# A ring of eight weight places instead of five, a stream of modulation weights loaded two ahead, and its dot products kept in program order up to the scan

## The chip, the cores and the metric

The kernel runs on one core of a Trainium2 chip. The core has a matrix engine (PE, TensorE), a vector engine (DVE), a scalar engine (ACT), GpSimd (POOL), and SyncE (SP), which in this kernel issues most DMA transfers. Each engine takes its instructions in the order of its own queue and waits on semaphores for the others. On-chip memory is SBUF, 128 partitions; matmul results go to PSUM.

The metric is the device time in microseconds of one execution; the median of several runs counts.

## The reference, cut to what matters

One layer on 256 latent tokens with 256 context tokens ahead of them, model width 2048: a modulated RMS norm, one wide projection that feeds latent attention (MLA, 8 heads) and a bidirectional gated DeltaNet (8 heads, chunks of 64), gates, an output projection, and then a gated convolution MLP (FFN).

```python
sh1, sc1, g1, sh2, sc2, g2 = jnp.split(jax.nn.silu(c) @ w_ada[l] + b_ada[l], 6, axis=-1)
...
(lq_a, lkv_a, lk_r, ldq, ldk, ldv, ldz, lda, ldb, lga, lgb) = split_columns(
    modulate(rmsnorm(x, norm_mix[l]), sh1, sc1) @ w_in[l])
...
y_mla_l = attend_latent(q_l, k_l, v_l, k_c, v_c)
...
o_dn_l, _ = dn_bidirectional(lq, lk, lv, lgd, lbeta, s_ctx, True)
y_l = merge_branches(y_mla_l, dn_output(o_dn_l, ldz, dn_o_norm[l], x.dtype), lga, lgb,
                     w_o_mla[l], w_o_dn[l], w_out[l])
x = x + jnp.expand_dims(g1, -2) * y_l
x = x + jnp.expand_dims(g2, -2) * conv_glu(
    modulate(rmsnorm(x, norm_ffn[l]), sh2, sc2), w_ffn_up[l], ffn_conv[l], w_ffn_down[l])
```

Of the six modulation vectors the first two are needed at once. The other four (g1, sh2, sc2, g2) are first needed behind the output projection. The change touches how these four are computed: 4 x 2048 dot products over 2048 inputs, 64 MB of weights.

## The kernel before

**Weights.** All weights come from HBM as float32 tiles of 128 x 1024 (512 KB) and are split in two parts for the matmul. `raw_w` (L125) takes a place of the ring "raw" (NR = 5 places of 4 KB per partition) and issues the load on SP. For each half of 512 columns `split` (L119) then makes `whi` by a cast on ACT (L121) and `wlo = raw - whi` on DVE (L122); both come from rings of NH = 6. PE multiplies with `whi` and `wlo` (all matmuls have the line of the wrapper, L68). A place of "raw" comes free when the last `wlo` of its tile is done; SP then issues the next load that has been waiting for a place.

**The late modulation.** `ada_rest` (L254) is a generator with 128 steps. Step i takes one tile `rawa` of in_wada from the same ring "raw", and one DVE instruction (L279) multiplies it by the activated conditioning vector `sch` and sums along the row into a column of `parts`. In the trace this instruction shows as CUSTOM_DVE_ANT_0, followed by a short read of the accumulator. The load of step i + 1 is issued ahead of the dot product of step i (`ahead = load(0)`, then `ahead = load(i + 1)`), so at most one load is ahead of the dot product in the traced program. Every 32 steps one of the four vectors is finished (`ada.done`).

The generator is wrapped in a `Side`, which is advanced by a budget in nanoseconds: each step costs 1300. The head phase calls `ada(c * ADB / 22600)` (L804), the attention `ada(AD * c)` (L1166, AD = 0.55), the scan `ada(ADS * c)` (L1375, ADS = 0.3), and the output projection and the FFN call it with further budgets.

**Phases by the trace.** Projections and the DeltaNet's heads with their short convolutions and triangular systems run until about 440 us, then the attention (four pairs of heads, `mla_project` and `mla_attend`) until about 720, the scan of the DeltaNet (eight steps) until about 930, the output of both branches with their gates and the output projection until about 1063, a short norm, and the FFN to the end. While one of these runs, PE's queue is filled with projection matmuls of other parts (gates, in_wgm and in_wgd, product `gtp`).

**What sets the order.** The program is traced in Python. `pe`, `oact`, `odve` and `osync` are wrappers (class `Ordered`, L58ff): an instruction issued through one of them while it is `pinned` keeps its place behind the instruction of that engine that was traced ahead of it. Instructions issued through the plain `act`, `dve`, `sync` can be placed elsewhere on their engine by a scheduler that works with its own estimates. L279 is issued through `dve`, so its place is the scheduler's choice.

**Names that the text uses.** In a head's normalisation `row_diag` (L175): `l2m` (norms, then a power on POOL, L173), `rb_h` and `rb_l` (high and low part, L179 and L180), `rb_d` (diagonal, L185), which the matmul `bp` needs. In the attention: `ks` (column sums of squares on PE), `km` (L1022, DVE), the softmax row maximum `s_`/`mns` (L1118 to L1122), `PT` (the transposed weights, split) and `yps` (values). `zx` are gate rows. In the scan: `S` (state; scaled on ACT at L1311, copied at L1322), `jit`, `tt`, `yraw` and `gt` (the scan's own loads).

Of the kernel before, what the change touches and what calls it, by code (L numbers as in the profile page):

```python
# [11 lines left out]
ALU = mybir.AluOpType  # L12
# [14 lines left out]
G3 = 96 + 256 * N1  # L27
GR = 1024
GH = 512
NR = 5  # L30
NH = 6
AD = 0.55
GD0 = 2
# [20 lines left out]
def hybrid_block(ctx: ExitStack, tc: tile.TileContext, io, dbg=None):  # L54
    nc = tc.nc
    act, dve, pool, sync = nc.scalar, nc.vector, nc.gpsimd, nc.sync
# [18 lines left out]
    pe, oact, odve = (Ordered(e) for e in (nc.tensor, nc.scalar, nc.vector))  # L75
# [27 lines left out]
    half = const.tile([P, 1], F32, name="half")  # L103
# [20 lines left out]
    def raw_w(src):  # L124
        n = src.shape[1]  # L125
        raw = wr.tile([P, GR], F32, tag="raw", name="raw", bufs=NR)[:, :n]
        sync.dma_start(raw, src)
# [126 lines left out]
    def ada_rest():  # L254


        def load(i):
            w = wr.tile([P, GR], F32, tag="raw", name="rawa", bufs=NR)
            c, n = divmod(i, 32)
            sync.dma_start(w, io["wada2"][c, (n // 16 + c) % 2, n % 16])  # L260
            return w

        parts = ad.tile([P, 2, 16], F32, name="parts")
        half, ahead = None, load(0)
        for i in range(128):
            c, n = divmod(i, 32)
            h, j = (n // 16 + c) % 2, n % 16
            if h != half:

                for _ in range(1 if i else 0):  # L270
                    yield 1300
                half, sch = h, ad.tile([P, GR], F32, tag="sch", name="sch")
                sync.dma_start(sch, Sc[h])
                for _ in range(3):
                    yield 1300
            w = ahead
            if i < 127:
                ahead = load(i + 1)
            dve.tensor_tensor_reduce(out=w, in0=w, in1=sch, scale=1.0, scalar=0.0, op0=ALU.mult, op1=ALU.add, accum_out=parts[:, h, j : j + 1])  # L279
            if n == 31:  # L280
                cs = slice(16 * c, 16 * c + 16)
                dve.tensor_tensor(out=adaT[:, cs], in0=parts[:, 0], in1=parts[:, 1], op=ALU.add)
                dve.tensor_tensor(out=adaT[:, cs], in0=adaT[:, cs], in1=bada[:, 32 + 16 * c : 48 + 16 * c], op=ALU.add)
                ada.done = c + 1
            yield 1300
# [43 lines left out]
    def load_shift(p):  # L329
        raws = []  # L330
        for m in range(4):
            raws.append(wr.tile([P, GR], F32, tag="raw", name="raw", bufs=NR))
            osync.dma_start(raws[m], io["wadab"][p, m])
# [76 lines left out]
    def load(*what):  # L410
        for kind, n in what:
            d, f = {"w": (wts, load_scale), "s": (shifts, load_shift), "g": (grs, load_first)}[kind]
            d[n] = f(n)
# [204 lines left out]
    for st in range(8):  # L618
        B = [pg2.tile([P, 8, 64], F32R, tag=f"B{n}", name="B") for n in range(2)]
        for n in range(2):  # L620
            dve.tensor_tensor(out=B[n], in0=mle64.unsqueeze(1).broadcast_to([P, 8, 64]),
                              in1=ghl[:, n, st].unsqueeze(2).broadcast_to([P, 8, 64]), op=ALU.mult)
# [147 lines left out]
    def head_inputs(h, side=lambda c: None):  # L770
        if h < N1:
            xs = [dkx[:, 2 * h], dkx[:, 2 * h + 1]]
        else:
            xs = []
            for w in ("wdk", "wdv"):
                pss = proj(io[w][h], (0, 1), side)
                x = pb2.tile([P, 2, T], F32, tag="cx", name="cx")
                for s in range(2):
                    gather(pss[s], P, x[:, s])
                xs.append(x)  # L780
        ps = proj(io["wdq"][h], (0,), side)[0]
        xq = pb2.tile([P, 1, T], F32, tag="cq", name="cq")
        gather(ps, P, xq[:, 0])
        return xs[0], xs[1], xq

    ada = Side(ada_rest())
    ada.done = 0
    ins = {h: head_inputs(h) for h in (3, 0)}

    def chains(*hs):  # L790
# [412 lines left out]
    def branch(w, wh, f, ymat, out):  # L1203

        if f % 4 == 0:
            gt = pd2.tile([P, 4, T], F32, tag="gt", name="gt")
            sync.dma_start(gt, Gs[wh, :, f : f + 4])
            gts[wh] = gt
        W = load_w(io[w][f])
        ps = psm.tile([P, 512], F32, tag="mm", name="brp")  # L1210
        for k in range(HEADS):
            mm_hl(ps, P, W(k * P), ymat[:, k], k == 0, k == HEADS - 1)
            if k == 3:
                yield 1300
        ox = pd2.tile([P, T], F32, tag="ox", name="ox")
        act.activation(ox, ps[:, T:], AF.Copy, scale=0.5)
        dve.scalar_tensor_tensor(out=ox, in0=ps[:, :T], scalar=0.5, in1=ox, op0=ALU.mult, op1=ALU.add)
        dve.scalar_tensor_tensor(out=out, in0=gts[wh][:, f % 4], scalar=1.0, in1=ox, op0=ALU.add, op1=ALU.mult)
        yield 1300
# [143 lines left out]
    def e_fill():  # L1363
        for f in range(KD):
            for n in range(4):
                c = next(gates, None)
                if c is not None:
                    yield c
            yield from branch("womla", 0, f, YM, t1[:, f])

    fill = Side(e_fill())
    pe.pinned = True
    for c in scan():
        fill(RE * c)
# [234 lines left out]
```

## Time and profile before

| what | value |
|---|---|
| median of 3 runs | 1796.3 us (1796.25 to 1796.43) |
| the profiled execution | 1796.66 us |
| its span | 1794.8 us |
| granted TensorE clock, mean | 0.988 |
| ACT's casts to whi (L121) | 940, 574.3 us |
| DVE's wlo (L122) | 940, 632.6 us |
| L279, dot products | 128, 155.8 us |
| HBM read and written | 388.57 MB and 28.84 MB |

The span runs from the first to the last instruction in the trace. The engines work side by side, so their busy times don't add up to it. A group of instructions in the profile is named by line, engine and operation, with output and inputs by the program's names; the number behind the bar is its busy time, the next the mean duration in ns, and behind the second bar stands the time for which the engine stood idle just before them and who ended that.

### The profile page before, as it was taken

To read this page: it belongs to the slowest core of one execution; us is meant where nothing else is said; L and a number is where in the kernel's file an instruction comes from. 1 tells how busy PE (TensorE), PEld (TensorE's weight loads), DVE (VectorE), ACT (ScalarE), POOL (GpSimd) and SP (SyncE) were. 2 spreads that over 40 slices of the span, in tenths; PEclk is the share of its full clock that TensorE was granted. 3 is DMA by queue.
4 is the path that set the end of the run, shared out by engine and by line. 5 is a ranking of instruction groups with operands and counts; after the bars stand their busy time and mean duration, and the time that the engine had idled before them with its cause. 6 is when DMAs were issued, how large, how long until landed. Compare 5 with 4: busy or idle time off the path is not lost.

```text
span 1794.8 us, 34114 instructions
## 1 busy us (share of the span) xinstructions
PE 1740.9 (97%) x12957; PEld 1504.6 (84%) x12957; DVE 1353.9 (75%) x2692; ACT 944.5 (53%) x1962; POOL 42.1 (2%) x49
## 2 busy tenths in 40 slices
PE   7999999999999999899999989999999999999999
PEld 6787888887888888687878878888888888888888
DVE  4687899879677777576789889887788888755554
ACT  3334544444567666564655546555555555544443
POOL 0000010000000000000010000000000000000000
PEclk9999999999899999999999989999999999999999
DMA  9982788773778767888957966777677777666663
GB/s 383 399 319 89 207 241 241 228 213 104 220 241 260 229 213 249 279 308 309 317 166 240 327 234 224 244 229 229 190 224 226 225 225 225 184 199 199 198 199 122
DMA packets 191493, 419.79 MB, mean 234 GB/s; under 512 B 57248, under 2 KB 97312, under 8 KB 188896
## 3 DMA queue, kind: packets, MB, share of 16 engines
q1 hardware_dynamic: 164144, 402.38, 69.0%
q10 hardware_dynamic: 27184, 15.23, 2.8%
q8 instruction: 102, 1.67, 0.4%
q14 instruction: 63, 0.52, 0.1%
HBM read 388.57 MB, written 28.84 MB: 233 GB/s over the span
## 4 chain that ended last, share of the span: by engine, by line
PE 70%; issue 10%; DMA 9%; DVE 6%; ACT 3%; POOL 1%; SPq 0%; POOLq 0%; DVEq 0%; ACTq 0%
PE fps L68 25%; PE dps L68 13%; PE mmp L68 9%; PE gtp L68 7%; PE fp L68 4%; DMA rawa<-in_wada 4%; DVE wlo L122 2%; PE brp L68 2%; DMA raw<-in_wadab 1%; PE amp L68 1%; DVE rawa L279 1%; DMA raw<-in_wgd 1%; ACT whi L121 1%; PE op L68 1%; DMA raw<-in_wz 1%
## 5 line engine op out<-in xcount | busy, mean ns | idle before, releaser
L122 DVE TENSOR_TENSOR wlo<-raw,whi 128x512 fp32r<-128x512 f32 (+1 forms) x940 | 632.6, 685 | 220.4 <-ACT whi L121 212.1
L121 ACT CAST whi<-raw 128x512 fp32r<-128x512 f32 (+1 forms) x940 | 574.3, 619 | 425.2 <-PE dps L68 113.7
L68 PE MATMUL fps<-H,whi 128*128 128x512 f32 x1376 | 475.1, 394 | 1.7 <-DVE H L1446 1.7
L68 PE MATMUL fps<-H,wlo 128*128 128x256 f32 x1376 | 372.3, 281 | 0.3 <-DVE wlo L122 0.3
L68 PEld LDWEIGHTS fps<-H,whi 128*128 128x128 f32 x1376 | 253.7, 189 | 53.3 <-issue 2.0
L68 PEld LDWEIGHTS fps<-H,wlo 128*128 128x128 f32 x1376 | 259.8, 189 | 7.8 <-DVE wlo L122 0.7
L68 PE MATMUL gtp<-h,whi 128*128 128x512 f32 x640 | 235.1, 404 | 7.4 <-ACT whi L121 7.1
L68 PE MATMUL mmp<-h,whi 128*128 128x512 f32 x640 | 227.1, 397 | 0.0
L68 PE MATMUL dps<-GB,whi 128*128 128x512 f32 (+1 forms) x595 | 195.7, 378 | 0.0
L279 DVE CUSTOM_DVE_ANT_0 rawa<-rawa,sch 128x1024 f32<-128x1024 f32 x128 | 155.8, 1220 | 45.5 <-DMA rawa<-in_wada 41.9
L68 PE MATMUL gtp<-h,wlo 128*128 128x256 f32 x640 | 176.0, 285 | 4.4 <-DVE wlo L122 4.2
L68 PE MATMUL mmp<-h,wlo 128*128 128x256 f32 x640 | 176.0, 281 | 0.6 <-DVE wlo L122 0.6
L68 PE MATMUL dps<-GB,wlo 128*128 128x256 f32 x560 | 154.1, 280 | 0.0
L68 PEld LDWEIGHTS gtp<-h,whi 128*128 128x128 f32 x640 | 121.8, 192 | 34.1 <-ACT whi L121 9.5
L68 PEld LDWEIGHTS mmp<-h,whi 128*128 128x128 f32 x640 | 119.0, 188 | 24.7 <-issue 0.4
L68 PEld LDWEIGHTS gtp<-h,wlo 128*128 128x128 f32 x640 | 122.9, 192 | 11.9 <-DVE wlo L122 7.5
L68 PEld LDWEIGHTS dps<-GB,whi 128*128 128x128 f32 x595 | 109.2, 188 | 21.1
L68 PEld LDWEIGHTS mmp<-h,wlo 128*128 128x128 f32 x640 | 120.3, 188 | 3.9 <-DVE wlo L122 1.3
L68 PEld LDWEIGHTS dps<-GB,wlo 128*128 128x128 f32 x560 | 105.1, 188 | 0.6
L68 PE MATMUL fp<-h,gh 128*128 128x256 f32 (+1 forms) x448 | 85.1, 290 | 2.5 <-ACT h L68 1.7
L68 PEld LDWEIGHTS fp<-h,gh 128*128 128x128 f32 (+1 forms) x448 | 69.4, 189 | 7.6 <-issue 4.1
L517 ACT COPY fx<-fps 128x256 f32<-128x256 f32 x86 | 31.8, 372 | 65.4 <-PE fps L68 65.3
(566 smaller groups left out, 2525.4 us busy)
## 6 DMA issues: line engine op xcount, KB each, us to landing
rawa<-in_wada SPq DMA_DIRECT2D x128, 512.0 KB, 4.7
raw<-in_wgate SPq DMA_DIRECT2D x82, 512.0 KB, 4.3
raw<-in_wval SPq DMA_DIRECT2D x82, 512.0 KB, 4.6
raw<-in_wdown SPq DMA_DIRECT2D x80, 512.0 KB, 4.3
wt<-in_wadas SPq DMA_DIRECT2D x16, 1024.0 KB, 10.8
raw<-in_wadab SPq DMA_DIRECT2D x32, 512.0 KB, 9.2
raw<-in_wgm SPq DMA_DIRECT2D x32, 512.0 KB, 4.7
raw<-in_wgd SPq DMA_DIRECT2D x32, 512.0 KB, 6.1
```

The costliest lines, as they stand in the source:

```text
L68: i = f(*a, **k)
L121: act.copy(hi, raw)
L122: dve.tensor_tensor(out=lo, in0=raw, in1=hi, op=ALU.subtract)
L279: dve.tensor_tensor_reduce(out=w, in0=w, in1=sch, scale=1.0, scalar=0.0, op0=ALU.mult, op1=ALU.add, accum_out=parts[:, h, j : j + 1])
L517: act.copy(out, ps[:M, T:])
```

## The change

The ring "raw" gets eight places (NR = 8). Room for them, 12 KB more per partition, comes from a scratch area that is cut to 1024 (`dynamic_dma_scratch_size`). `ada_rest` starts with two loads and keeps two ahead of the dot product. The dot product goes through `odve` while `ada.bound` is true, that is until the line just ahead of the scan's loop, and through `dve` from there on. The line numbers behind the last edits move by one.

```diff
-NR = 5
+NR = 8
...
-        half, ahead = None, load(0)
+        half, ahead = None, [load(0), load(1)]
...
-            w = ahead
-            if i < 127:
-                ahead = load(i + 1)
-            dve.tensor_tensor_reduce(out=w, in0=w, in1=sch, ...)
+            w = ahead.pop(0)
+            if i < 126:
+                ahead.append(load(i + 2))
+            (odve if ada.bound else dve).tensor_tensor_reduce(out=w, in0=w, in1=sch, ...)
...
-    ada.done = 0
+    ada.done, ada.bound = 0, True
...
     fill = Side(e_fill())
+    ada.bound = False
     pe.pinned = True
     for c in scan():
...
-    nc = bacc.Bacc("TRN2", target_bir_lowering=False, num_devices=1)
+    nc = bacc.Bacc("TRN2", target_bir_lowering=False, num_devices=1, dynamic_dma_scratch_size=1024)
```

The change moves instructions on DVE, ACT and SP; every engine has the same instructions as before, and PE's order is the same but for seven small places. Three places follow, each with the rows of before first.

**DVE in the attention, second pair of heads, ahead of the first km.** Each row is a line, an operation, output and inputs, and the shape; a dot product is the row ISA rawa,parts (L279 before, L68 where it goes through the wrapper), with its short second part behind it.

```order
L518 TENSOR_TENSOR zx<-gtp,zx 128x256
L279 ISA rawa,parts<-rawa,sch 128x1024
L279 ISA parts 128x1
L917 SCALAR_TENSOR_TENSOR zx<-zt,zx 128x256
L122 TENSOR_TENSOR wlo<-raw,whi 128x512
L1118 ISA s__6299,mns<-kbc,sps 128x512
L1118 ISA mns 128x1
L122 TENSOR_TENSOR wlo<-raw,whi 128x512
L1120 TENSOR_SCALAR mns<-mns,qm 128x1
L279 ISA rawa,parts<-rawa,sch 128x1024
L279 ISA parts 128x1
L1022 SCALAR_TENSOR_TENSOR km<-ks,krm 128x4
```

```order
L518 TENSOR_TENSOR zx<-gtp,zx 128x256
L122 TENSOR_TENSOR wlo<-raw,whi 128x512
L917 SCALAR_TENSOR_TENSOR zx<-zt,zx 128x256
L122 TENSOR_TENSOR wlo<-raw,whi 128x512
L1118 ISA s__6301,mns<-kbc,sps 128x512
L1118 ISA mns 128x1
L1120 TENSOR_SCALAR mns<-mns,qm 128x1
L1022 SCALAR_TENSOR_TENSOR km<-ks,krm 128x4
L990 CAST rb_h<-km 128x4
L1122 RECIPROCAL mns<-mns 128x1
```

Before, one dot product stands behind the first zx and one directly ahead of km. Now none stands in this stretch, and the next one follows behind the reciprocal and km. Just ahead of the stretch there were three dot products between the first wlo and the reciprocal, two of them next to each other, and there are two now.

**SP and ACT at the entry to the scan.** SP's loads of in_wgd (gate weights), in_womla and in_wada, the stores Ys of the attention and the first of the scan's own loads (jit):

```order
L127 DMA raw<-in_wgd 128x1024 x6
L127 DMA raw<-in_womla 128x1024
L1140 DMA Ys<-ryx 128x256
L260 DMA rawa<-in_wada 128x1024
L1238 DMA jit<-KTs 128x1024
L1140 DMA Ys<-ryx 128x256
L1239 DMA jit<-Vs 128x1024
```

```order
L127 DMA raw<-in_wgd 128x1024 x6
L127 DMA raw<-in_womla 128x1024
L1140 DMA Ys<-ryx 128x256
L260 DMA rawa<-in_wada 128x1024
L127 DMA raw<-in_wgd 128x1024
L1140 DMA Ys<-ryx 128x256
L1238 DMA jit<-KTs 128x1024
L1239 DMA jit<-Vs 128x1024
```

One more load of in_wgd stands ahead of the scan's loads. The load that has moved there stood behind all of the scan's first loads, in a pair.

ACT from the scan's first y to the casts of gate weights behind the first state copies:

```order
L1293 COPY y<-yp 128x512 x2
L1216 ACTIVATE ox<-brp 128x256
L1322 COPY S<-sp__8999 128x4x128
L1322 COPY S<-sp__9000 128x4x128
L1322 COPY S<-sp__9011 128x4x128
L1322 COPY S<-sp__9012 128x4x128
L121 CAST whi<-raw 128x512 x6
```

```order
L1293 COPY y<-yp 128x512 x2
L1216 ACTIVATE ox<-brp 128x256
L1322 COPY S<-sp__9001 128x4x128
L1322 COPY S<-sp__9002 128x4x128
L1322 COPY S<-sp__9013 128x4x128
L1322 COPY S<-sp__9014 128x4x128
L121 CAST whi<-raw 128x512 x4
```

Two of the six casts have moved ahead of these rows. Further on, the next two casts stood between the thirteenth and the fourteenth of sixteen scalings of S (L1311) and now stand behind all sixteen.

**DVE in the attention, ahead of a PT of the second pair.** From a gate row to PT:

```order
L518 TENSOR_TENSOR zx<-gtp,zx 128x256
L122 TENSOR_TENSOR wlo<-raw,whi 128x512
L279 ISA rawa,parts<-rawa,sch 128x1024
L279 ISA parts 128x1
L518 TENSOR_TENSOR qx<-qps,qx 128x256
L122 TENSOR_TENSOR wlo<-raw,whi 128x512 x3
L122 TENSOR_TENSOR PT<-ptp,PT 128x4x128
```

```order
L68 ISA rawa,parts<-rawa,sch 128x1024
L68 ISA parts 128x1
L518 TENSOR_TENSOR qx<-qps,qx 128x256
L282 TENSOR_TENSOR adaT<-parts 128x16
L122 TENSOR_TENSOR wlo<-raw,whi 128x512
L283 TENSOR_TENSOR adaT<-adaT,vecs 128x16
L68 ISA rawa,parts<-rawa,sch 128x1024
L68 ISA parts 128x1
L122 TENSOR_TENSOR wlo<-raw,whi 128x512
L68 ISA rawa,parts<-rawa,sch 128x1024
L68 ISA parts 128x1
L122 TENSOR_TENSOR PT<-ptp,PT 128x4x128
```

Where one dot product and four wlo stood, there are now three dot products and two wlo (the two adds of 128x16 finish one of the four vectors).

More of the change, by code (lines that the diff above doesn't have):

```diff
@@ L275, in ada_rest @@
                     yield 1300
-            w = ahead
-            if i < 127:
-                ahead = load(i + 1)
-            dve.tensor_tensor_reduce(out=w, in0=w, in1=sch, scale=1.0, scalar=0.0, op0=ALU.mult, op1=ALU.add, accum_out=parts[:, h, j : j + 1])
+            w = ahead.pop(0)
+            if i < 126:
+                ahead.append(load(i + 2))
+            (odve if ada.bound else dve).tensor_tensor_reduce(out=w, in0=w, in1=sch, scale=1.0, scalar=0.0, op0=ALU.mult, op1=ALU.add, accum_out=parts[:, h, j : j + 1])
             if n == 31:
```

## The prediction

> **What bounds the kernel now.** I read the page first, then a table of stretches, then the time line of every place where PE stands idle. From the page:
>
> ```profile
> span 1794.8 us, 34114 instructions
> PE 1740.9 (97%) x12957; PEld 1504.6 (84%) x12957; DVE 1353.9 (75%) x2692; ACT 944.5 (53%) x1962; POOL 42.1 (2%) x49
> L279 DVE CUSTOM_DVE_ANT_0 rawa<-rawa,sch 128x1024 f32<-128x1024 f32 x128 | 155.8, 1220 | 45.5 <-DMA rawa<-in_wada 41.9
> ```
>
> PE is busy for 1740.9 of 1794.8 us, so everything that this change can give lies in the other 53.9 us and in what PE does at a reduced clock; its work stays the same. The profiled execution took 1796.66 us, its span is 1794.8, and the median of the runs is 1796.3; I sum against 1796.66 and take off 0.36 at the end. The third row is the bait: the dot products (L279) wait 41.9 us for their tiles. Whether that is worth anything depends on whether PE waits behind them.
>
> The stretches (start:end; length, then busy time and instructions of PE, PEld, DVE, ACT, POOL; granted clock, DMA share, GB/s):
>
> ```profile
> 0.00:60.00 60.00, 48.02 (x514) 36.08 (x514) 30.20 (x51) 20.85 (x39) 2.29 (x10) 0.94 0.98 391
> 125.00:440.00 315.00, 310.67 (x2672) 263.69 (x2671) 266.84 (x571) 149.42 (x312) 20.28 (x20) 1.00 0.66 195
> 440.00:720.00 280.00, 267.62 (x1957) 232.69 (x1957) 211.41 (x458) 178.25 (x401) 14.24 (x14) 0.97 0.73 229
> 720.00:930.00 210.00, 194.36 (x2101) 163.32 (x2101) 146.32 (x304) 116.84 (x278) 4.57 (x4) 0.98 0.84 288
> 1050.00:1080.00 30.00, 24.10 (x164) 21.34 (x163) 21.60 (x45) 13.50 (x28) 0.70 (x1) 0.83 0.50 170
> 1080.00:1795.00 715.00, 711.29 (x4136) 626.51 (x4134) 517.49 (x962) 374.39 (x708) 0.00 (x0) 1.00 0.67 210
> ```
>
> In the first 60 us the DMA engines are at 0.98: a longer ring brings no bytes sooner there, and SP's order is unchanged. From 1080 on PE is busy 711.29 of 715, and the rest is its last drain: nothing to gain in 40% of the kernel. What is open is 4.3 us of idle PE in the head phase (125 to 440), 12.4 in the attention (440 to 720), 15.6 in the scan (720 to 930) and 5.9 at the boundary to the FFN, 38 us together, and only those parts of it that wait for a weight tile or stand behind a dot product.
>
> **The attention: one place pays.** DVE's and PE's time lines (start, us, engine, line, operation; in brackets the idle time before and who ended it):
>
> ```profile
> 515.86 0.43 PE L68 MATMUL ks<-ones,ksq 128*32 128x1 f32 x32
> 516.89 1.22 DVE L279 CUSTOM_DVE_ANT_0 rawa<-rawa,sch 128x1024 f32<-128x1024 f32 x1 [3.20 <-DMA rawa<-in_wada]
> 518.98 0.68 DVE L1118 CUSTOM_DVE_ANT_0 s__6299<-kbc,sps 128x512 f32<-128x512 f32 x1
> 520.32 1.21 DVE L279 CUSTOM_DVE_ANT_0 rawa<-rawa,sch 128x1024 f32<-128x1024 f32 x1
> 521.46 0.15 DVE L1022 SCALAR_TENSOR_TENSOR km<-ks,krm 128x4 f32<-128x4 f32 x1
> 521.67 0.60 PE L68 MATMUL ks<-ones,ksq 128*32 128x1 f32 x32 [3.75 <-DVE km L1022]
> ```
>
> DVE stands 3.20 us in front of a dot product whose tile was issued too late, runs it, and runs a second dot before km; PE's next column sum waits 3.75 us for km. In the changed order no dot product stands between the second zx and km. Ahead of km there go the wait of 3.20 and two dots of about 1.15 each (the distance from a dot's start to the next instruction, 520.32 to 521.46), 5.5 us; as many wlo as before stay. That puts km at 521.46 - 5.5 = 516.0, and its input, the column sum of 515.86, ends at 516.3: km at about 516.4, ahead of the point where PE stopped (517.92 = 521.67 - 3.75). The gap of 3.75 goes.
>
> Its clock goes with it. The same kind of table on a grid of 3.413 us:
>
> ```profile
> 517.06:520.47 3.41, 0.86 (x8) 0.65 (x6) 3.41 (x9) 1.68 (x6) 0.00 (x0) 1.00 0.83 268
> 520.47:523.88 3.41, 2.21 (x40) 2.20 (x41) 3.08 (x9) 3.35 (x7) 1.37 (x2) 0.50 0.97 342
> 523.88:527.30 3.42, 3.42 (x14) 3.03 (x14) 2.97 (x7) 0.37 (x1) 0.95 (x1) 0.50 0.93 304
> 735.51:738.92 3.41, 1.58 (x30) 1.39 (x26) 0.85 (x2) 2.07 (x5) 0.00 (x0) 1.00 0.93 324
> 844.74:848.15 3.41, 1.68 (x13) 1.11 (x10) 3.41 (x10) 1.14 (x3) 0.00 (x0) 1.00 0.65 171
> 848.15:851.56 3.41, 3.41 (x12) 2.89 (x11) 1.90 (x4) 0.00 (x0) 0.00 (x0) 0.50 0.84 226
> 1063.19:1066.60 3.41, 0.42 (x28) 0.34 (x32) 2.56 (x5) 1.65 (x3) 0.00 (x0) 1.00 0.81 253
> ```
>
> A stretch in which PE was busy 0.86 of 3.41 us is followed by two at a clock of 0.50. In those PE worked 2.21 + 3.42 = 5.63 us at half speed, which at full speed are 2.8. So **A = -3.75 - 2.8 = -6.6 us**. From below: if the dot that now stands ahead of the first mns (a place earlier) still waits 3.20, nothing goes; from above nothing more is there than the 6.6.
>
> [...]
>
> The other waits of the dots in the attention I cost at nothing: I followed PE's other gaps over 1 us there back, and none has a waiting dot ahead of its releaser; PE's own queue of projection matmuls hides those waits. Where that cover is thin, a gap changes sign:
>
> ```profile
> DVE rawa L279 <- DMA rawa<-in_wada: 41.9, 35, 4.2
> 712.76 1.44 PE L68 MATMUL yps<-PT,V 128*128 128x512 f32 x7 [1.87 <-DVE PT L122]
> ```
>
> The first row is used below. In the gap of the second a dot comes ahead of PT in the changed order where a wlo stood, 1.15 for 0.6 (the distance of two wlo): **E = +0.5**, bounds 0 and +1.15.
>
> **Scan entry.** ACT, SP and PE:
>
> ```profile
> 739.36 3.65 ACT L121 CAST whi<-raw 128x512 fp32r<-128x512 f32 x6 [1.08 <-DMA raw<-in_wgd]
> 734.34 0.85 SPq L127 DMA_DIRECT2D raw<-in_wgd  x2
> 740.03 0.49 PE L68 MATMUL gtp<-h,whi 128*128 128x512 f32 x1 [2.94 <-ACT whi L121]
> 748.64 2.45 ACT L1311 ACTIVATE S<-S,dec 128x128 f32<-128x128 f32 x8
> 753.36 0.49 PE L68 MATMUL gtp<-h,whi 128*128 128x512 f32 x1 [2.14 <-ACT whi L121]
> ```
>
> The tile was issued behind the scan's own loads and landed late. In the changed order one load of in_wgd goes ahead of them and two whi casts ahead of the scan's first copies, so PE finds the tile: -2.94. But three S scalings (2.45 / 8 = 0.31 each) have moved ahead of the casts that the gap of 2.14 waits for: +0.93. **B = -2.0**; bounds 0 (the 1.25 us or so of that tile's transfer only moved, and the scan's DMA share is 0.84) and -2.94. The rest of the scan stays: there raw loads stand behind small loads that wait for earlier landings, not for a place in the ring.
>
> **The boundary.**
>
> ```profile
> 1064.25 1.26 ACT L121 CAST whi<-raw 128x512 fp32r<-128x512 f32 x2 [1.36 <-DMA raw<-in_wgate]
> 1064.89 0.69 DVE L122 TENSOR_TENSOR wlo<-raw,whi 128x512 fp32r<-128x512 f32 x1 [0.84 <-ACT whi L121]
> 1066.49 0.35 PE L68 MATMUL ss<-ones,x1q 128*32 128x1 f32 x16 [2.67 <-ACT x1q L1419]
> ```
>
> The order is unchanged here; with eight places the tile of in_wgate is there, ACT's wait goes, and with it DVE's 0.84 that stands ahead of the last x: **C = -0.9**. From above -2.6, if the half-clock stretch behind it is a window of 3.41 us shorter (-1.7); from below 0.
>
> **Head phase.**
>
> ```profile
> 289.08 1.22 DVE L279 CUSTOM_DVE_ANT_0 rawa<-rawa,sch 128x1024 f32<-128x1024 f32 x1
> 290.86 0.63 PE L68 MATMUL bp<-rb_d,onesr 128*128 128x256 f32 x2 [1.02 <-ACT whi L121]
> 305.35 1.22 DVE L279 CUSTOM_DVE_ANT_0 rawa<-rawa,sch 128x1024 f32<-128x1024 f32 x1
> 307.40 1.00 PE L68 MATMUL bp<-rb_d,onesr 128*128 128x512 f32 x2 [0.48 <-DVE rb_d L185]
> ```
>
> Both dots run between the halves of rb, and PE waits for rb_d. In the changed order a wlo stands for the first (1.15 - 0.6 = 0.55 less) and nothing for the second (0.48 gone): **D = -1.0**, bounds 0 and -1.5.
>
> **What the binding costs.** A bound dot can't be taken forward into an idle spot of DVE, so dots come in clusters. The sharpest cluster stands ahead of a PT:
>
> ```profile
> 560.76 0.69 DVE L122 TENSOR_TENSOR PT<-ptp,PT 128x512 fp32r<-128x512 f32 x1 [1.01 <-ACT PT L121]
> 563.54 1.58 PE L68 MATMUL yps<-PT,V 128*128 128x512 f32 x8
> ```
>
> Three dots instead of one, two wlo less: 2 x 1.15 - 2 x 0.6 = 1.1, against 1.01 us that DVE stood idle there, and 2.1 us from the end of PT (561.45) to the matmul that needs it (563.54). It hides, if the tiles have landed; behind a waiting dot stand PT, the rotation (L1085ff) and, through them, PE. I can't do this for each of the roughly 70 dots that are bound in view of such a chain: bounds 0 and +4, taken as **+2.0**, about one gap of the sizes seen above (1.87, 2.14). A longer ring itself costs nothing on an engine; the loads are the same in number and size.
>
> **Sum:** -6.6 - 2.0 - 0.9 - 1.0 + 0.5 + 2.0 = -8.0; 1796.66 - 8.0 - 0.36 = **1788.3 us**. Windows of half clock that the shift moves onto or off a gap are 1.7 us apiece either way; with the bounds the forecast's own range is 1783.5 to 1793.
>
> **Rivals.**
> 1. *The dots' waits vanish, PE doesn't notice.* If A fails because the dot at the earlier place still waits for its landing (3.20), only B to D less the new stalls are left: -2.0 - 0.9 - 1.0 + 2.5 = -1.4, 1794.9. For it: 41.9 us of waits, one gap over 3 us. Against: no dot stands in the last stretch ahead of km.
> 2. *Slower: the cluster ahead of PT waits.* Three dots in 3.5 us need three tiles that have landed; two loads are ahead, so the third may wait up to the longest seen, 4.2. It decides from a wait over 2.1 us: PE then stands 4.2 - 2.1 = 2.1 us and loses a window (1.7), 3.8 per place. With A not earned either (the same late tile) B to E are left, -3.4: two places give 7.6 - 3.4 = +4.2, 1800.5, and four +11.8, 1808. One place alone decides nothing. Against: eight places hold more landed tiles than five.
> 3. *It doesn't do what it says:* SP waits elsewhere than at the ring.
>
> ```profile
> SPq L127 <- DVE wlo L122: 621.6, 326, 19.3
> SPq L1248 <- DMA Gs<-zx: 23.3, 6, 5.4
> ```
>
> The first row (us, times, longest) is the wait for a ring place; the second is a wait of another kind, 23.3 us in the scan. Were that kind decisive everywhere, B and C fail and A rests on the order alone: A + D + E + 2.0 = -6.6 - 1.0 + 0.5 + 2.0 = -5.1, 1791.2. But 621.6 against 23.3 says that it is the ring, outside the scan.
>
> **Chances.** Forecast 0.60 (faster by over 0.2%, that is 3.6 us, about what a measurement of this kernel can tell from no change), rival 3 0.12 (faster), rival 1 0.19 (within 0.2%), rival 2 0.09 (slower). Faster 0.72, same 0.19, slower 0.09. The range takes in rivals 1 and 3 and the bounds: 1783.5 to 1796.0.
>
> **What would show it.** Right: the gap of 3.75 ahead of ks and the 0.50 clock near 520 are gone; the wait in front of L279 falls from 41.9 to under 15; the 2.94 gap at the first gtp of the scan is under 0.5 and the 2.14 one near 3; the FFN's length is unchanged. Wrong: a new PE gap whose releaser is PT, qt, km or rb_d with an L279 ahead of it, or a km that is still late.

## The result, and the profile after

| | before | changed |
|---|---|---|
| median | 1796.75 us (8 runs) | 1786.06 us (8 runs, 1783.0 to 1790.97) |
| ratio | | 0.9944, 95% interval 0.9932 to 0.9956 |
| profiled execution, its span | 1796.66, 1794.8 us | 1783.0, 1781.2 us |
| clock of the profiled execution | 0.988 | 0.992 |

The kernel became 10.7 us faster; 8.0 were forecast against the median shown before (1796.3). One of the eight runs of before took 1906.24 us and stays out of the ratio; the median of the other seven is 1796.43. The profiled execution is the shortest of its eight, so its 13.6 us against the profile of before are more than the change is worth, and the first thing to learn from the two traces is how much more, and why.

The page of the changed kernel; the dot products now have two lines, since up to the scan they go through the wrapper (L68):

```profile
span 1781.2 us, 34182 instructions
PE 1733.8 (97%) x12957; PEld 1499.9 (84%) x12957; DVE 1354.3 (76%) x2692; ACT 948.9 (53%) x1962; POOL 42.8 (2%) x49
L279 DVE CUSTOM_DVE_ANT_0 rawa<-rawa,sch 128x1024 f32<-128x1024 f32 x68 | 83.1, 1222 | 22.2 <-DMA rawa<-in_wada 21.2 <-DMA sch<-Sc 0.7
L68 DVE CUSTOM_DVE_ANT_0 rawa<-rawa,sch 128x1024 f32<-128x1024 f32 x60 | 72.9, 1218 | 0.0
```

The 60 bound dots never wait: 0.0 us. DVE's wait ahead of dots fell from 41.9 to 21.2 us, and all of the rest is behind the point where the binding ends.

Since both traces have the same 12957 matmuls in nearly the same order, I cut them at the same matmuls and take from each piece PE's idle time between its first and its last matmul, and half of what PE was busy at a clock of 0.50. The half is an estimate of the loss against full clock, and a little high: a pair of gtp's matmuls, whi and wlo, starts every 0.64 us at 0.50 (743.27 to 745.83 in the changed trace) and every 0.35 at 1.00 (847.38 to 848.08 before). The changes in length sum up to the difference of the spans; the two columns ahead of them explain most of each, not all. The forecast's +2.0 for new stalls has no place of its own and stands in no row:

| piece, by the trace of before (us) | idle, slow clock before | idle, slow clock after | change in length | forecast |
|---|---|---|---|---|
| start and heads, to 440 | 12.1, 2.8 | 13.1, 3.4 | +0.8 | D -1.0 |
| first kv tiles, 440 to 469 | 4.5, 4.9 | 4.8, 0.7 | -3.5 | 0 |
| second pair, 469 to 528 | 3.8, 2.8 | 0.0, 0.0 | -6.3 | A -6.6 |
| rest of the attention, to 700 | 2.2, 0.0 | 0.0, 0.0 | -3.4 | 0 |
| last values, 700 to 715 | 1.9, 0.0 | 3.0, 1.7 | +2.7 | E +0.5 |
| scan entry, 715 to 757 | 5.5, 0.0 | 3.4, 1.7 | -0.3 | B -2.0 |
| scan, 757 to 852 | 6.4, 1.7 | 5.4, 0.0 | -2.8 | 0 |
| scan's end and its norm, to 934 | 3.7, 1.7 | 5.1, 3.1 | +3.0 | 0 |
| output projection, boundary, to 1075 | 6.0, 3.1 | 3.6, 1.4 | -4.3 | C -0.9 |
| first FFN tiles, to 1093 | 0.0, 0.7 | 1.4, 0.0 | +1.0 | 0 |
| FFN | 0.3, 0.0 | 0.0, 0.0 | -0.4 | 0 |

The place of the largest term, on DVE's time line (start, us, engine, line, operation, idle time before):

```profile
511.82 0.69 DVE L1118 CUSTOM_DVE_ANT_0 s__6301<-kbc,sps 128x512 f32<-128x512 f32 x1 [0.83 <-PE sps L68]
513.62 0.16 DVE L1022 SCALAR_TENSOR_TENSOR km<-ks,krm 128x4 f32<-128x4 f32 x1 [0.85 <-PE ks L68]
515.12 1.21 DVE L68 CUSTOM_DVE_ANT_0 rawa<-rawa,sch 128x1024 f32<-128x1024 f32 x1
```

DVE now waits for PE in front of km (0.85) where PE waited for DVE (3.75), and the dot comes behind. PE's other gaps of the changed kernel, from its time line:

```profile
283.42 0.43 PE L68 MATMUL sp<-ones,sqk 128*32 128x1 f32 x32 [1.42 <-ACT sqk L672]
701.55 1.75 PE L68 MATMUL yps<-PT,V 128*128 128x512 f32 x5 [3.03 <-DVE PT L122]
730.66 0.51 PE L68 MATMUL gtp<-h,whi 128*128 128x512 f32 x1 [0.26 <-ACT whi L121]
741.81 0.49 PE L68 MATMUL gtp<-h,whi 128*128 128x512 f32 x1 [2.73 <-ACT whi L121]
911.38 1.10 PE L68 MATMUL obp<-rb_d,onesr 128*128 128x512 f32 x2 [1.31 <-DVE rb_d L185]
1053.72 0.31 PE L68 MATMUL ss<-ones,x1q 128*32 128x1 f32 x16 [0.79 <-ACT x1q L1420]
1077.11 0.47 PE L68 MATMUL fps<-H,whi 128*128 128x512 f32 x1 [1.37 <-DVE H L1447]
```

The rows are, in order: a new gap in the heads; the gap ahead of the last values, 1.87 before; the scan's first gate tile, 2.94 before; its second, 2.14 before; a new gap at the scan's end; the boundary, 2.67 before, where the 0.47 ahead of it is gone too; and a new gap at the start of the FFN, where an unbound dot runs ahead of H.

### The profile page after: what moved, and what is told of

It reads as the page before. It is cut to its first block, busy times and chain, and to the rows that moved or that the text cites. A ratio compares the mean times of both kernels' runs of the same rounds, so it can differ in the third digit from the quotient of the medians.

```text
span 1781.2 us, 34182 instructions
## 1 busy us (share of the span) xinstructions
PE 1733.8 (97%) x12957; PEld 1499.9 (84%) x12957; DVE 1354.3 (76%) x2692; ACT 948.9 (53%) x1962; POOL 42.8 (2%) x49
## 4 chain that ended last, share of the span: by engine, by line
PE 60%; issue 8%; DVE 3%; DMA 2%; ACT 1%; POOL 0%; SPq 0%; POOLq 0%; ACTq 0%; DVEq 0%
PE fps L68 27%; PE dps L68 13%; PE gtp L68 10%; PE brp L68 2%; PE vps L68 1%; PE kps L68 1%; DVE wlo L122 1%; PE ivp L68 1%; PE sps L68 1%; PE qps L68 1%; PE op L68 1%; PE kp L68 1%; DMA raw<-in_wgd 0%; PE yps L68 0%; ACT whi L121 0%
## 5 line engine op out<-in xcount | busy, mean ns | idle before, releaser
L68 PE MATMUL fps<-H,whi 128*128 128x512 f32 x1376 | 473.7, 393 | 3.1 <-DVE H L1447 3.1
L68 PE MATMUL fps<-H,wlo 128*128 128x256 f32 x1376 | 371.8, 280 | 0.0
L68 PEld LDWEIGHTS fps<-H,whi 128*128 128x128 f32 x1376 | 253.1, 188 | 54.5 <-issue 1.9
L68 PEld LDWEIGHTS fps<-H,wlo 128*128 128x128 f32 x1376 | 259.1, 188 | 7.5 <-DVE wlo L122 0.5
L68 PE MATMUL gtp<-h,whi 128*128 128x512 f32 x640 | 232.9, 401 | 5.0 <-ACT whi L121 4.7
L68 PE MATMUL mmp<-h,whi 128*128 128x512 f32 x640 | 226.7, 397 | 0.0
L68 PE MATMUL dps<-GB,whi 128*128 128x512 f32 (+1 forms) x595 | 195.7, 378 | 0.0
L68 PE MATMUL gtp<-h,wlo 128*128 128x256 f32 x640 | 175.2, 284 | 3.6 <-DVE wlo L122 3.6
L68 PE MATMUL mmp<-h,wlo 128*128 128x256 f32 x640 | 175.9, 281 | 0.0
L68 PE MATMUL dps<-GB,wlo 128*128 128x256 f32 x560 | 154.1, 280 | 0.0
L68 PEld LDWEIGHTS gtp<-h,whi 128*128 128x128 f32 x640 | 120.8, 190 | 31.4 <-ACT whi L121 7.1
L68 PEld LDWEIGHTS mmp<-h,whi 128*128 128x128 f32 x640 | 119.0, 188 | 24.4 <-ACT dkx L529 0.3
L68 PEld LDWEIGHTS gtp<-h,wlo 128*128 128x128 f32 x640 | 121.7, 190 | 10.8 <-DVE wlo L122 6.5
L68 PEld LDWEIGHTS dps<-GB,whi 128*128 128x128 f32 x595 | 109.2, 188 | 21.1
L68 PEld LDWEIGHTS mmp<-h,wlo 128*128 128x128 f32 x640 | 120.3, 188 | 3.1 <-issue 1.0
L68 PEld LDWEIGHTS dps<-GB,wlo 128*128 128x128 f32 x560 | 105.1, 188 | 0.6
L279 DVE CUSTOM_DVE_ANT_0 rawa<-rawa,sch 128x1024 f32<-128x1024 f32 x68 | 83.1, 1222 | 22.2 <-DMA rawa<-in_wada 21.2
L68 PE MATMUL fp<-h,gh 128*128 128x256 f32 (+1 forms) x448 | 84.8, 290 | 2.5 <-ACT h L68 1.7
L68 PEld LDWEIGHTS fp<-h,gh 128*128 128x128 f32 (+1 forms) x448 | 69.1, 188 | 7.6 <-issue 4.1
L68 DVE CUSTOM_DVE_ANT_0 rawa<-rawa,sch 128x1024 f32<-128x1024 f32 x60 | 72.9, 1218 | 0.0
```

The costliest lines, as they stand in the source:

```text
L68: i = f(*a, **k)
L279: (odve if ada.bound else dve).tensor_tensor_reduce(out=w, in0=w, in1=sch, scale=1.0, scalar=0.0, op0=ALU.mult, op1=ALU.add, accum_out=par ...
```

## The experiments

All kernels are variants of the changed one. "Held" is the mean time from the issue of a tile of in_wada to its dot, for the dots between 440 and 720 us of each trace; "left" is the number of places of the ring less those that such tiles held, counted from issue to the end of the dot and averaged over the same 280 us (for two rings, the places of the weights). The expectations below reckon the places held as dots times held, divided by 280 us; that takes in time ahead of 440 us and comes out too high: 3.5 for the ring of three places in e5, where the count gives 2.9. "Span x clock" is the median over the runs of each run's span times its mean clock: the same runs with part of the scatter taken out (over the 20 runs of before the standard deviation falls from 3.6 to 2.5 us; one step in the clock's third digit is 1.8 us).

The runs came in three series on three chips, each with its own runs of before, to which the ratios refer: 1795.8 us (20 runs, span x clock 1771.8) for e1 to e4, 1795.34 (23, 1773.9) for e5 to e8, 1797.34 (32, 1773.0) for e9 to e12.

| kernel | places | loads ahead | bound to | median us (runs) | ratio to before, 95% interval | span x clock | held us | left |
|---|---|---|---|---|---|---|---|---|
| before, first series | 5 | 1 | - | 1795.8 (20) | 1 | 1771.8 | 5.8 | 3.9 |
| changed, e1 | 8 | 2 | scan | 1788.24 (8) | 0.9954, 0.9935 to 0.9973 | 1764.1 | 29.1 | 3.7 |
| e2 | 8 | 1 | - | 1796.53 (12) | 1.0005, 0.9984 to 1.0025 | 1772.7 | 5.8 | 6.9 |
| e3 | 5 | 1 | scan | 1809.29 (6) | 1.0082, 1.0054 to 1.0109 | 1782.5 | 17.6 | 2.3 |
| e4 | 8 | 1 | scan | 1783.68 (7) | 0.9941, 0.9917 to 0.9965 | 1764.3 | 24.2 | 4.2 |
| e5 | 5 + 3 | 1 | scan | 1815.04 (5) | 1.0114, 1.0092 to 1.0136 | 1781.9 | 22.0 | 5 |
| e6 | 6 + 2 | 1 | scan | 1813.03 (5) | 1.0100, 1.0080 to 1.0121 | 1780.7 | 14.0 | 6 |
| e7 | 6 | 1 | scan | 1800.86 (12) | 1.0030, 1.0013 to 1.0047 | 1776.0 | 20.0 | 2.9 |
| e8 | 8 | 2 | - | 1795.41 (12) | 0.9999, 0.9985 to 1.0014 | 1772.3 | 6.1 | 6.8 |
| e9 | 6 + 2 | 1 | end | 1796.62 (12) | 0.9991, 0.9975 to 1.0007 | 1773.0 | 14.3 | 6 |
| e10 | 8 | 1 | end | 1795.47 (12) | 0.9981, 0.9959 to 1.0003 | 1770.3 | 24.9 | 4.1 |
| e11 | 7 | 1 | scan | 1791.37 (12) | 0.9968, 0.9949 to 0.9987 | 1767.4 | 22.2 | 3.5 |
| e12, as e4 | 8 | 1 | scan | 1788.30 (9) | 0.9948, 0.9925 to 0.9970 | 1764.7 | 24.4 | 4.2 |

**e1: the changed kernel again.** No edit.

> The changed kernel a second time. Its eight executions so far lie 8 us apart (1783.0 to 1790.97), those of before, but for one, 1.4 us (1796.25 to 1797.64). [...] Theory D (landings): the gaps themselves differ by 1 us or more from profile to profile because tiles land earlier or later, and the half-clock stretches follow. Both expect a median near 1786.

Theory D fails in the main: the gaps came again. The second profile (1784.46 us) has the gaps of the first within 0.1 us at the last values (3.07 against 3.03), the scan's second gate tile (2.73 both) and the FFN's start (1.37 both); of those over 1 us two differ by more than 0.3: 1.13 instead of 1.74 ahead of a wlo at 834 us, and 0.71 instead of 1.18 at 150 us. The loss at half clock differs where the gaps do not: 3.4 us instead of 0.7 in the piece from 440 to 469, 5.2 instead of 3.1 at the scan's end. So most of the -3.5 us of that piece in the first table is a matter of the execution, not of the change: in the second profile the piece is 1.1 us shorter than before.

One gap with a stretch at half clock behind it and without is seen in e4 and e12, which are one kernel. The table of stretches, cut in intervals of 3.413 us, at whose edges the clock changes in the traces of before and changed, e4 first, then e12 (start:end; length, busy time of PE, PEld, DVE, ACT, POOL, granted clock, DMA share, GB/s):

```profile
696.98:700.40 3.42, 1.63 (x9) 1.45 (x10) 2.33 (x4) 0.85 (x3) 0.00 (x0) 1.00 0.86 260
700.40:703.81 3.41, 3.41 (x22) 2.98 (x21) 2.94 (x6) 1.62 (x3) 0.52 (x1) 1.00 0.95 319
```

```profile
700.68:704.09 3.41, 1.38 (x8) 1.24 (x9) 2.58 (x5) 1.10 (x3) 0.00 (x0) 1.00 0.69 232
704.09:707.51 3.42, 3.42 (x12) 2.83 (x11) 2.54 (x4) 0.97 (x2) 0.52 (x1) 0.50 0.92 333
```

Both have a gap of 2.23 us ahead of the last values. In e4 1.79 us of it fall into one interval, PE is busy 1.63 of 3.42 us there, and the clock stays at 1.00; in e12 2.03 us of it fall into one interval, PE is busy 1.38 of 3.41 us, and the next one runs at 0.50.

**e2: eight places alone.**

```diff
-        half, ahead = None, [load(0), load(1)]
+        half, ahead = None, [load(0)]
-            if i < 126:
-                ahead.append(load(i + 2))
+            if i < 127:
+                ahead.append(load(i + 1))
-    ada.done, ada.bound = 0, True
+    ada.done, ada.bound = 0, False
```

> Eight places alone; one load ahead, dot products unbound. Theory P (the prediction's): the gap of 3.75 us ahead of ks is the work of the dots that the scheduler took forward; in this kernel's order the late one between the two zx is gone but one still stands just ahead of km, so the gap falls to 1.2 us or less, and its half clock goes if it is under 1.5; the tile at the boundary to the FFN is there (gaps of 0.47 and 2.67 fall by 2 us or more together); the scan's entry keeps its 2.94 us gap, since in_wgd still stands behind the scan's loads. 1796.5 - 5 - 3 = about 1788.5. Theory B (the binding does it): ring alone gives under 3 us, 1793.5 or more, with the gap ahead of ks still over 2 us.

The time is that of before, as Theory B put it, though gaps closed: at the boundary 2.67 became 0.79, as Theory P said; ahead of ks 3.75 became 1.80 (at the matmul behind it), where Theory P said 1.2 or less (its 1.5 us for the clock is an estimate, from 844.74 to 848.15 before, where PE stood idle 1.73 of 3.41 us and 0.50 followed; no run shows it as a limit); and the gaps of 2.94 and 2.14 ahead of the scan's first two gate tiles, which it said would stay, are gone too. The profiled execution, 1787.15 us, is the fastest of its twelve, so its trace shows more gain than the median. Neither theory expected the rest. The page's group of dots and three rows of DVE and PE:

```profile
L279 DVE CUSTOM_DVE_ANT_0 rawa<-rawa,sch 128x1024 f32<-128x1024 f32 x128 | 156.2, 1222 | 54.8 <-DMA rawa<-in_wada 50.5 <-DMA sch<-Sc 2.2 <-DMA masks<-in_masks 1.2
...
603.35 1.23 DVE L279 CUSTOM_DVE_ANT_0 rawa<-rawa,sch 128x1024 f32<-128x1024 f32 x1 [1.35 <-DMA rawa<-in_wada]
604.84 0.68 DVE L122 TENSOR_TENSOR PT<-ptp,PT 128x512 fp32r<-128x512 f32 x1
605.58 0.50 PE L68 MATMUL qps<-qan__4746,whi 128*128 128x512 f32 x1 [1.87 <-DVE PT L122]
```

With a longer ring the wait ahead of the dots rises, from 41.9 to 50.5 us. The tile is held 5.8 us as before: wherever its load goes, the scheduler puts an unbound dot right behind it, and DVE waits for the landing with PT, km or a head's norm behind it. Other new gaps are 2.42 at 281 us in the heads and 2.24 at 448 ahead of the first kps.

**e3: the binding alone.** As the changed kernel, but `NR = 5` and one load ahead as in e2.

> The binding alone; five places, one load ahead. Theory P: no dot stands between the second row maximum and km, so the gap ahead of ks is under 1 us and its half clock gone (-6); the boundary to the FFN keeps its 2.67 us gap, since it waits for a place in the ring; at the scan's entry more gate loads stand ahead of the scan's loads than before, so the 2.94 us gap falls too. 1790 +- 2. Theory R (the ring does it): with five places the dots land as late as before; bound, they wait in front of the chain somewhere else, PE gets another gap of 2 us or more ahead of PT, qt or ks, and the time is 1794 or more.

Slower by 13.5 us. The dots do wait less: 9.6 us in all, against 41.9, and the 60 bound ones 0.0. The weight tiles pay. By the pieces of the first table this trace, 10.5 us longer than before, loses most in the heads (7.0 us; up to 450 us ACT waits 24.0 us there for weight tiles, none before), between 528 and 700 us (6.1) and at the scan's entry (5.6). In the order by waits (us, times, longest), and on the time lines of SP, ACT and PE at the scan's entry:

```profile
ACT whi L121 <- DMA raw<-in_wgm: 22.4, 16, 3.0
```

```profile
744.85 0.38 SPq L127 DMA_DIRECT2D raw<-in_womla  x1
749.74 1.14 ACT L121 CAST whi<-raw 128x512 fp32r<-128x512 f32 x2 [6.19 <-DMA raw<-in_womla]
750.41 0.80 PE L68 MATMUL brp<-YM,whi 128*128 128x512 f32 x1 [9.12 <-ACT whi L121]
```

A bound dot keeps its place in the program, but its load was issued long ahead, so its tile stands in the ring for 17.6 us instead of 5.8, and that with only five places. Both theories were wrong on where it shows: not ahead of PT or qt, but in ACT's casts, which wait for gate tiles (there is no such wait for in_wgm before), and at the scan's entry, where the first load of in_womla now stands behind all of the scan's first loads.

**e4: eight places and the binding, one load ahead.** As the changed kernel, with one load ahead as in e2.

> Eight places and the binding, one load ahead: the change without its second load. Theory P: the second load ahead does nothing of its own, because with eight places and the order of the loads set by the scheduler a tile lands long before its dot; the time is that of the changed kernel within its scatter, 1784 to 1789, and DVE's wait ahead of L279 is within 5 us of the changed kernel's. Rival: the second load is what lets bound dots find their tiles; without it the wait ahead of L279 is 10 us or more above the changed kernel's and the time 1790 or more.

As Theory P, 0.3 us under its range: 1783.68 us, the changed kernel's time within the scatter, and span x clock the same (1764.3 and 1764.1). The wait ahead of the dots is 25.6 us against 21.2 and 19.6.

**e5 and e6: two rings.** Weights 5 and in_wada 3 places, or 6 and 2; otherwise as e4.

```diff
-            w = wr.tile([P, GR], F32, tag="raw", name="rawa", bufs=NR)
+            w = wr.tile([P, GR], F32, tag="rawa", name="rawa", bufs=3)
```

> Bound dots, one load ahead, and two rings instead of one: five places for the weight tiles, three of their own for the tiles of in_wada; eight places in all, as in the changed kernel. Theory O (occupation): a bound dot holds its place long (from issue to dot 17.6 us on average between 440 and 720 us with five shared places and 24.2 with eight, against 5.8 unbound), so 45 such tiles in 280 us take 2.8 of five and 4.0 of eight places, and binding with five slows the weight tiles, not the dots. With a ring of their own the tiles of in_wada can't take more than three, the weights have their five back, and the time is that of eight places with binding, 1780 to 1789 (median near 1784); ACT's waits for raw tiles stay under those of the binding alone (in_wgm 22.4 us, in_wz 12.2). Theory L (length): what counts is that any tile can be eight loads ahead; weights with five places wait at the boundary to the FFN and at the scan's entry as before, +3 to +5: 1787 to 1792.

> The same with six places for weights and two for in_wada. Theory O: two places are enough if the tile has landed when its bound dot comes (one waits, one loads): the time is 1780 to 1789 again, and the weights with six places gain or equal e5. Theory L: less far ahead for the dots, more for the weights: the wait ahead of L279 and its bound form rises by 10 us or more over the 25.6 us of eight shared places, and the time is above that of e5 by 3 us or more.

Both expectations failed, and by far: 1815 and 1813 us. Up to the scan Theory O is right: the trace of e6 is 11.6 us ahead of before at the scan's first gate tile (the changed one 12.7). Behind it the lead is lost and more: e6 is 13.4 us behind at the start of the FFN. The dots by stretch, before first, then e6 (busy time and number of L279's instructions on DVE; clock, DMA share, GB/s of the stretch):

```profile
720.00:930.00 210.00, 24.21 (x20) 0.98 0.84 288
1060.00:1120.00 60.00, 3.38 (x3) 0.91 0.60 195
```

```profile
720.00:930.00 210.00, 35.32 (x29) 0.93 0.87 304
1060.00:1120.00 60.00, 12.20 (x10) 0.89 0.75 241
```

```profile
1074.31 1.23 DVE L279 CUSTOM_DVE_ANT_0 rawa<-rawa,sch 128x1024 f32<-128x1024 f32 x1 [2.61 <-DMA sch<-Sc]
1076.44 0.39 PE L68 MATMUL ss<-ones,x1q 128*32 128x1 f32 x16 [5.72 <-ACT x1q L1420]
```

With a ring of their own the loads of in_wada no longer stand in line with the weights. From the scan on the dots are unbound, and 29 instead of 20 of them come into the scan and 10 instead of 3 between 1060 and 1120 us, onto DVE's chains: at the boundary a dot stands waiting for its vector in front of the last x, and PE waits 5.72 us. That the shared ring had held them back is tested in e9.

**e7: binding with six places.** As e4 with `NR = 6`.

> Binding with six shared places, one load ahead. Theory O: between the binding with five (1809) and with eight (1784); about 2.8 to 3.2 places held by tiles of in_wada leave some 3 for the weights, so half or more of the loss is gone: 1790 to 1798, with ACT's wait for in_wgm tiles in the attention under half of the 22.4 us with five, and the 9.12 us gap at the scan's entry gone or under 4, since the load of in_womla there has a place earlier. Rival: the 1809 came from another order at the scan's entry that the binding brings, whatever the number of places; then the gap of 9 us stays and the time is 1803 or more.

1800.86 us, between five and eight places, where Theory O put it up to 1798: a third of the loss is gone, not half. ACT's wait for in_wgm is 14.3 us, not under 11.2, and the 9.12 gap is gone.

**e8: eight places, two loads ahead, unbound.** As the changed kernel, with `ada.bound` false from the start.

> Eight places and two loads ahead, dots unbound: the change without the binding. Theory O: unbound dots are put right behind their landing by the scheduler (5.8 us from issue to dot, with five places and with eight), so a second load ahead and more places leave the dot where it waits: DVE's wait ahead of L279 is 40 us or more, and the time that of eight places alone, 1796 +- 3. Rival: the second load ahead is what the longer ring was missing; the wait falls under 25 us and the time to 1790 or less.

As Theory O: 1795.41 us, held 6.1 us, wait ahead of the dots 53.8 us.

**e9: e6 with the dots bound to the end.** The line `ada.bound = False` is taken out.

> Six places for weights and two for in_wada as in e6, but the dots bound to the end of the program, not only up to the scan. The trace of e6 was 11.6 us ahead of the kernel before at 740 us and 13.4 behind at 1090; 29 dots ran in the scan (20 before) and 10 between 1060 and 1120 us (3 before). Theory U (unbound dots): with a ring of their own nothing holds back the loads of in_wada from the scan on, and the scheduler puts the dots right behind them, on DVE's chains; bound, they keep to their places, the loss behind 740 goes, and the time is 1782 to 1790. Theory L (too few places for weights behind the attention: six instead of eight): binding changes nothing there, 1805 or more.

1796.62 us: the binding takes back 16.4 us of e6's loss, of the 29.4 by which it stood above e4 (24.7 above e12). In its trace 21 dots run in the scan and 6 between 1060 and 1120 us, and the gap of 5.72 is 0.79. So over half of the loss was the unbound dots, and Theory L falls as it was put; but the time is 6.6 us over the upper end of Theory U's range. In this trace the lead of 8.4 us at the scan's first gate tile still goes in the scan. What costs there with six places wasn't separated from the held tiles.

**e10: e4 with the dots bound to the end.** The same line is taken out.

> Eight shared places, one load ahead, dots bound to the end. Theory O: in the scan the tiles of in_wada are then held longer (10.7 us unbound) and take places from the gate and output weights that the scan and the output projection need; the scan's entry and steps get gaps of 2 us or more ahead of gtp and brp, and the time is 1787 to 1797, above e4. Rival: the bound dots stay out of the scan's own DVE chains, the time is that of e4 or up to 3 us less, 1780 to 1785.

As Theory O: 1795.47 us, 7 to 12 above e12 and e4. In the scan the tiles of in_wada are held 24.7 us (10.7 in e4), and the scan's gates wait:

```profile
731.14 0.80 PE L68 MATMUL gtp<-h,whi 128*128 128x512 f32 x1 [3.65 <-ACT whi L121]
```

**e11: binding with seven places.**

> Binding with seven shared places, one load ahead. Theory O: places left for the weights in the attention (places less tiles of in_wada held on average) were 2.2 with five (1809), 2.8 with six (1801), 4.0 with eight (1784), 4.1 before the change; with seven some 3.5, which by the line through these gives 1790 to 1794. Rival: a threshold, seven already as good as eight: 1786 or less; or as bad as six: 1798 or more.

1791.37 us, as Theory O by the line through five, six and eight places. The largest gap of its trace, 4.16 us ahead of the last values, stands behind a wait of ACT for a weight tile (in_wgd, 1.98 us).

**e12: e4 again.** No edit.

> The same kernel as e4 a second time: the change without the second load ahead. Theory O: without the second load the tiles of in_wada hold 4.0 places of eight on average instead of 4.9, which the weights get; its time is again at or under that of the changed kernel (1786.06 and 1788.24 in two series), 1782 to 1787. Rival: e4's median was chance; 1787 to 1790, and the second load ahead does nothing either way.

1788.30 us, against 1783.68 the first time. Its median is over Theory O's range and in that of the rival; its span x clock is e4's within the step of the clock (1764.7, 1764.3), so the two series differ mainly by the clock (medians 0.988 and 0.990). The second load ahead does nothing that these runs can show, and no version here beats the changed kernel beyond the scatter.

## Why the prediction was right, point by point

- **The time** was right: 1788.3 forecast, 1786.06 measured in the first series and 1788.24 in the second, and the sign. In part that is luck: only A, some 60% of the 10.7 us, came as it was worked out; the terms B, C and E missed by 1.7 to 3.4 us, with both signs, and pieces put at nothing moved by -3.5 to +3.0. The range of 1783.5 to 1793 was also narrower than the terms' own bounds, which reach from 1782.7 (all at their best) to about 1801 (all at their worst).
- **A, -6.6, was right** in place, size and clock: -6.3 in that piece. The wait of 3.20 went with the order that the binding keeps: the 60 bound dots wait 0.0 us here, as they do with one load ahead (e4) and with five places (e3), while the ring alone (e2) left a gap of 1.80 behind km. The places were needed for something else. In e3 PE stands 3.08 us near that place, behind ACT, which waits for a weight tile:

```profile
521.24 1.14 ACT L121 CAST whi<-raw 128x512 fp32r<-128x512 f32 x2 [3.26 <-DMA raw<-in_wz]
523.70 0.58 PE L68 MATMUL vps<-whi,kvn 128*128 128x256 f32 x1 [3.08 <-ACT bd L873]
```

- **C, -0.9, was mis-sized:** -4.3. The tile was there as said, but the step took DVE's idle 0.84 for the delay, while the whole row of whi, wlo, x and x1q hung on ACT's wait of 1.36, and x now comes at 1052.73, ahead of the end of PE's work. The gaps of 0.47 and 2.67 fell together by 2.4, and the slow clock behind them from 3.1 to 1.4 us, which was named only as an upper end.
- **B, -2.0, was mis-sized:** -0.3. The first gap went (2.94 to 0.26) and the second grew (2.14 to 2.73) as forecast; the failed step is the sum's silence on the clock there: 2.32 of the 2.73 us fall into one interval of 3.413 us (739.49 to 742.90, PE busy 0.86), and the next runs at 0.50, 1.7 us by the half of the first table, while before an edge between two intervals split both gaps (1.83 and 1.11 us, 1.36 and 0.78) and the clock stayed at 1.00. The 1.25 us in the bound of 0 are an estimate: 512 KB at 419 GB/s, the rate from 742.34 to 745.75 before.
- **E, +0.5, was mis-sized:** +2.7. The step let the dot replace a wlo, but between the two PT ahead of that gap three wlo stand before and after, so the dot comes on top: 1.87 + 1.15 = 3.02, and 3.03 was measured. (In e4 two wlo are left there, and the gap is 2.23.) It also brought an interval at 0.50:

```profile
698.53:701.94 3.41, 0.39 (x2) 0.35 (x3) 3.41 (x7) 1.55 (x4) 0.00 (x0) 1.00 0.71 208
701.94:705.36 3.42, 3.42 (x13) 2.94 (x12) 0.92 (x3) 0.37 (x1) 0.53 (x1) 0.50 0.89 272
```

- **D, -1.0, can't be read off its piece,** which is 0.8 us longer in this profile and 1.8 shorter in the second one; 1.2 of the 2.6 us between them lie ahead of 35 us. At its own place, 284 to 315 us, both profiles give -0.6: the gap of 1.02 fell to 0.48 as worked out and the one of 0.48 went, but ahead of the next bp one of 0.73 is new, which the step did not look for. At 283 us, outside that place, PE now waits 1.42 us for sqk. A bound dot at 274 us runs ahead of the convolution steps that end in it, and DVE's rows have changed places too; e2 waits 2.42 there with unbound dots, so the binding isn't shown to be the cause.
- **The new stalls, +2.0,** are 1.42 at sqk, 1.31 at the scan's end and 1.37 at the FFN's start, 4.1 in all, just over the upper end of +4, and they aren't what the term was for. All three stand in e2 as well (2.42, 1.41, 1.37), where no dot is bound; no dot runs close ahead of the 1.31, and the one ahead of the 1.37 is unbound.
- **"The other waits in the attention I cost at nothing"** failed on the good side: 3.4 us went between 528 and 700, 2.2 of it in idle time: the gaps of 0.84, 0.66 and 0.62 us there are gone, all under the 1 us down to which I had followed them. The other 1.2 us are not explained.
- **"A longer ring itself costs nothing on an engine"** failed as an account of why. Alone it gives back all it earns (e2): the scheduler put waiting dots ahead of other chains. And **"what the binding costs"**, bounds 0 and +4, is too narrow for the binding by itself: with five places it is +13.5 (e3). The two parts are worth -10.7 together (-7.6 to -12.1 over the series, with one load ahead or two) because each takes away what the other costs: the binding keeps dots from waiting at the head of DVE's queue, and the places pay for the tiles that then stand and wait.
- **The wait ahead of the dots** fell to 21.2, not under 15: the unbound dots from the scan on were left out of that number.

## What to carry to other kernels

An instruction that a scheduler places freely may be put right behind its load, as here, and then a longer ring only moves the wait; pinning it moves the wait from the engine into the ring, as places held, so count places as loads per time times the time each is held before pinning anything. A shared ring is also a brake: give one stream a ring of its own and its instructions, if they are free to move, come earlier, onto chains that had been free of them. Where the granted clock changes within the program, as it did here, judge a change by several executions and by span times clock: a gap of 2.23 us had 3.42 us at 0.50 behind it in one execution here (e12) and none in another (e4).

## What the runs showed of the hardware that was not expected

- In the traces of before and changed the granted clock is 1.00 or 0.50, and it changes at the edges of intervals of 3.413 us: those at 448.79 and 1076.84 before lie 184 intervals apart. Between 36 and 1120 us there are six stretches at 0.50 in each trace, of one to three intervals before (the longest from 1066.60 to 1076.84) and of one each in the changed kernel. Where the edges lie against the program differs from execution to execution: one kernel with one gap of 2.23 us had an interval of 3.42 us at 0.50 behind it, some 1.7 us by the half of the first table, in one execution and none in another (e12, e4). The 12 runs of e2 lie 17 us apart (1787.15 to 1804.31), the 32 of before in the last series 21. They follow the clock in part: span and clock correlate at -0.85 over e2's runs, at -0.78 over the 20 of before in the first series and at -0.33 over the 8 of e1.
- PE's busy time in an interval goes with the clock of the next one in part. Of the intervals at 1.00 between 36 and 1120 us of these two traces, all 7 with PE busy under 1.5 of 3.41 us were followed by 0.50; of 5 with 1.5 to 1.85 it was two (844.74 before, 1.68 us, was and 735.51 before, 1.58 us, was not); of 24 with 1.85 to 2.6 it was two, both at the scan's end (916.41 before, 903.33 changed); of the other 583 it was one (435.70 changed, 2.99 us). Each of these last three holds 64 to 128 matmuls of 128x1; whether that has to do with it stays open.
- The left-over places order the kernels with one shared ring that are bound up to the scan: 2.3, 2.9, 3.5 and 4.2 left for 1809, 1801, 1791 and 1784 to 1788 us. The changed kernel, with 3.7 left and 1786 to 1788 us, fits in: its second load holds half a place more than e4 (4.3 against 3.8). The order holds for these kernels alone: unbound, 3.9 and 6.9 places left both go with 1796 us (before, e2).
